# Two blocks on one core: a bias table's route, the split of a normed x, a gate's slots, and a pacing rate

## The chip, the cores and the metric

One of the eight cores of a Trainium2 chip runs the whole program in one launch. The metric is the device time of one execution in microseconds, as the median of several executions. Profiles show one execution, and their times count from the span's start.

## What is computed

`reference(...)` applies two transformer-like blocks to x of 256 tokens by 2048 features, all in float32.

```python
def reference(...):
    x = first_block(x, ...)      # mLSTM and gated delta rule side by side, gates, out projection, residual, rmsnorm
    return second_block(x, ...)  # below

def second_block(x, c, ctx, c_ctx, norm_g, w_mod, b_mod, w_in, w_out, lam_..., subln_g, rpb, final_g):
    shift, scale, gate = jnp.split(jax.nn.silu(c) @ wm + bm, 3, axis=-1)
    shift_c, scale_c = jnp.split(jax.nn.silu(c_ctx) @ wm[:, :2 * D_MODEL] + bm[:2 * D_MODEL], 2, axis=-1)
    hx = rmsnorm(h, norm_g[layer]) * (1.0 + scale[:, None]) + shift[:, None]
    hc = rmsnorm(ctx, norm_g[layer]) * (1.0 + scale_c) + shift_c
    qa, ka, va, ga, qb, kb, vb, gb = jnp.split(hx @ wi, 8, axis=-1)
    ...                                   # keys and values of hc too
    oa = diff_attention(...) * jax.nn.silu(ga)
    ob = neighbourhood_attention(..., rpb[layer], rows) * jax.nn.silu(gb)
    mixed = jnp.concatenate([oa, ob], axis=-1) @ w_out[layer]
    h = h + gate[:, None] * mixed
    return rmsnorm(h, final_g)
```

`hx` and `hc` have 256 rows each. `diff_attention` has 8 heads, each with two softmaxes; `neighbourhood_attention` has 8 heads and adds a bias by relative position, of 15 x 31 numbers per head (`rpb`).

## The kernel before

**Numbers and products.** Each float32 matrix is split into a high part in a reduced format and the low rest, `lo = w - hi`; a product is three matmuls, hi x hi, hi x lo, lo x hi. A weight tile is 512 KB (128 partitions of 1024 numbers). `load_w` loads it on SP's queue into one of four slots (pool wraw), and `split_w` makes `hi` with an ACT copy (line 139) and `lo` with a DVE subtraction (line 140) in three slots each (pool wsp). `proj` (line 161) multiplies eight weight tiles into a pair of PSUM banks (pool psA, two buffers), `proj_T` (line 145) does so for transposed results.

**Order.** The kernel is written in Tile: the code gives operations with priorities in their order of writing, and a planner puts them into each engine's in-order stream when their data and slots are there in its own timeline. Work written later fills gaps, so projections of the next stage run among the attention of the present one. `split_w` is raised in priority by 100. After each split `split_w` calls `tick[0]`, a hook that writes some side work at that point.

**Modulation.** The vectors shift, scale, gate need `silu(c) @ w_mod`, 12 column groups of 16 k tiles. `mod_step(i)` (line 460) is one of 192 steps: a load of 256 KB (line 463; for the last 64 on SP's queue) and a DVE multiply-add into a running sum (line 473). `mods(rate, upto)` (line 498) makes a hook that writes `rate` steps for each weight tile; `mods_all(upto)` writes what is still missing up to a number. The last 64 steps, the gate's, run in a ring of four slots and four sums, `mr`, and are paced from the first query tile of the neighbourhood attention on, at 1.6 a tile (line 1368). The four output columns of the last projection each call `mods_all(128 + 16 * (n + 1))` and `gate_row(n)`, which adds the sum over partitions with a matmul (`ms`, line 492), before column n is finished.

**Block 2's x.** After block 1, x lies as `hf[n]` (n = 0 to 3, 512 columns each, 256 rows). For each n, ACT scales it by the row norm (`xs`, line 941), PE transposes it in tiles of 128 (`ps`, line 945), and `mod_T` (line 857) applies scale and shift: ACT writes the high part `hxh` from PSUM, DVE writes the full value back to `hf[n]` from PSUM, and DVE (odd k) or POOL (even k) subtracts to give `hxl`. `value0` (line 988) then projects the values of hc and hx with `proj`, while `s_steps` (line 998) forms sums and differences of `hx` and `hc` quarters for a Strassen scheme, on DVE and ACT. `keys` (line 1048) uses these: it loads four weight tiles, forms differences of them on DVE (lines 1071 to 1074) and runs seven products; its first result goes to a scratch tile `tm` (line 1068).

**The bias table.** `rpb` is 8 rows of 465 numbers. It is loaded on POOL's queue to a tile `rb` of 8 partitions, one of two slots with the tag `tm`, and copied to DRAM as `rep`, 64 copies of every row (lines 971 to 973), from which `near_bias` (line 1299) later reads skewed windows. The other `tm` slot goes to `lq`.

**Attention.** `diff_attn(g, ...)` is called for two groups of four heads. `scores` writes two exponentials per head into a ring `er` of eight tiles of 512 columns; the next head's scores are written ahead of this head's `pv`. At the fourth unit it calls `gate2(g, "a")`, a projection with eight weight tiles whose result is turned into the gate `G` in a slot of its own (pool a2, one buffer); `out_T` transposes `G` at the end. `near_attn` follows with two groups, `gate2(g, "b")`, and writes `mb`, which takes the slot of `er`.

Of the kernel before, what the change touches and what calls it, by code (L numbers as in the profile page):

```python
# [9 lines left out]
F32 = mybir.dt.float32  # L10
F32R = mybir.dt.float32r
AF = mybir.ActivationFunctionType
ALU = mybir.AluOpType
# [3 lines left out]
P = 128  # L17
D = 2048
T = 256
# [65 lines left out]
def hybrid_block_kernel(  # L85
# [4 lines left out]
    act, ve, pe, gp = nc.scalar, nc.vector, nc.tensor, nc.gpsimd  # L90
# [29 lines left out]
    tick, last_lo = [None], [None]  # L120
# [79 lines left out]
    with ExitStack() as b1:  # L200
# [17 lines left out]
        with ExitStack() as s0:  # L218
# [64 lines left out]
            for w in range(2):  # L283
                for j in (1, 3):
                    for h in range(2):
                        hl = load_w(d["dn_qkv"][J0[w] + j, h], 8, P)
                        o = ps0[w][:, j // 2, j % 2, :]
# [20 lines left out]
            for n in range(4):  # L308
                full = pro.tile([P, 4, T], F32, tag="full", name="full", bufs=2)
                k4 = slice(4 * n, 4 * n + 4)  # L310
# [29 lines left out]
        with s1:  # L340
            nc.sync.dma_start(raws, d["if_ba"])
            ps = side([P, T], name="ps")[0:48]
            for h in range(2):
                hi, lo = split_w(raws[:, h * 8:(h + 1) * 8, :], 8, 48)
# [22 lines left out]
            e = gpool.tile([P, 2, 24], F32, name="e")  # L367
# [75 lines left out]
        for i, nm in enumerate(("c", "c_ctx")):  # L443
            o = VEC[nm]
# [3 lines left out]
        modT = cb1.tile([P, 4, KT], F32, name="modT")  # L448
# [49 lines left out]
        def mods(rate, upto):  # L498

            def f():  # L500
                mod_next[1] += rate
                while mod_next[1] >= 1.0:
                    mod_next[1] -= 1.0
                    if mod_next[0] < upto:
                        mod_step(mod_next[0])
                        mod_next[0] += 1
            return f
# [11 lines left out]
        with ExitStack() as s2:  # L519
# [38 lines left out]
            G = dn.tile([64, 8, 64], F32, name="G")  # L558
# [5 lines left out]
            for hg in range(4):  # L564
                vv, ww = (dn.tile([P, 2, 4, P], F32, tag=nm, name=nm) for nm in ("vv", "ww"))
                kq = dk.tile([P, 4, 2, T], F32, tag="kq", name="kq")
                ps = kps0 if hg == 0 else proj_T(d["dn_qkv"], 16 + 4 * hg, 4, U)
                rows = rsb if hg == 0 else None
                conv_silu(ps, 16 + 4 * hg, kq[:, :, 0, :], rows)
                ps = qps0 if hg == 0 else proj_T(d["dn_qkv"], 4 * hg, 4, U)  # L570
# [23 lines left out]
                for h in range(4):  # L594
                    g = 4 * hg + h
# [27 lines left out]
                for j in range(BASE - 1, 0, -1):  # L623
                    sh = [64, j, BASE - j]
# [9 lines left out]
                ps = proj_T(d["dn_qkv"], 32 + 4 * hg, 4, U)  # L634
# [19 lines left out]
                for q in range(4):  # L654
                    for i in range(8):
                        pe.matmul(cps[q % 2][Q[q], i, :], W[Q[q], i, :], Xd[Q[q], i, :], start=True, stop=True)
                    r = slice(32 * q, 32 * q + 16)
# [64 lines left out]
                st = sm1.tile([P, 2, 4], F32, tag="st", name="st")  # L722
# [23 lines left out]
        with ExitStack() as s3:  # L746
# [3 lines left out]
            for hg in range(2):  # L750
                kq = dk.tile([P, 4, 2, T], F32, tag="kq", name="kq")
                kT, qT = kq[:, :, 0, :], kq[:, :, 1, :]
                ps = proj_T(d["ml_k"], 4 * hg, 4, U)
                act.activation(kT, ps.rearrange("p a b t -> p (a b) t"), AF.Copy)  # L754
                ps = proj_T(d["ml_q"], 4 * hg, 4, U)
                act.activation(qT, ps.rearrange("p a b t -> p (a b) t"), AF.Copy, scale=P ** -0.5)
                for hp_ in range(2):
                    W0 = dk.tile([P, 2, T], F32, tag="W", name="W0")
                    W1 = ml.tile([P, 2, P], F32, tag="W1", name="W1")
                    for i in range(2):  # L760
                        h = 4 * hg + 2 * hp_ + i
# [54 lines left out]
                    for b in range(2):  # L816
# [4 lines left out]
                        for j in range(2):  # L821
                            k = 4 * (2 * hg + hp_) + 2 * b + j
# [10 lines left out]
        hf = [hfp.tile([P, 2, 512], F32, tag="hf", name="hf", bufs=4) for _ in range(4)]  # L833
# [3 lines left out]
        with ExitStack() as s4:  # L837
            o1 = s4.enter_context(tc.tile_pool(name="o1", bufs=2, reuse_waits="tile"))
            modp[0] = o1
            tick[0] = mods(0.55, 128)  # L840
            for n in range(4):
                gpp = proj(d["gate_a"], n, U)[0]
                act.activation(hf[n], gpp, AF.Tanh, scale=0.5)
            for n in range(4):
                gpp = proj(d["gate_b"], n, U)[0]
                act.activation(tb[:, :, n, :], gpp, AF.Tanh, scale=0.5)

            mods_all(128)
            tick[0] = None
            hch = big.tile([P, KT, T], F32R, tag="Ah", name="hch")  # L850
            hcl = big.tile([P, KT, T], F32R, tag="Al", name="hcl")
            gx = cb1.tile([P, 2, KT], F32, name="gx")
            og = VEC["norm_g"]
            for v in range(2):
                ve.scalar_tensor_tensor(gx[:, v, :], modT[:, 2 * v + 1, :], 1.0, vecT[:, og:og + 16], ALU.add, ALU.mult)

            def mod_T(ps, k, hi, lo, full):

                g, sh = gx[:, 0, k:k + 1], modT[:, 0, k:k + 1]
                act.activation(hi, ps, AF.Identity, scale=g, bias=sh)  # L860
                ve.tensor_scalar(full, ps, g, sh, ALU.mult, ALU.add)
                (ve if k % 2 else gp).tensor_tensor(lo, full, hi.bitcast(F32), ALU.subtract)

            for n in range(4):
                yp = proj(d["out_a"], n, [(hah, hal)])[0]
                ve.scalar_tensor_tensor(hf[n], hf[n], 1.0, yp, ALU.add, ALU.mult)
# [4 lines left out]
        with ExitStack() as s4:  # L871
# [66 lines left out]
            for n in range(4):  # L938
                xs = o1.tile([P, 2, 512], F32, tag="xr", name="xs")
                for t in range(2):  # L940
                    act.activation(xs[:, t, :], hf[n][:, t, :], AF.Copy, scale=rr[:, t:t + 1])
                for kk in range(4):
                    ps = side([P, T], name="ps")
                    for t in range(2):
                        pe.transpose(ps[:, t * P:(t + 1) * P], xs[:, t, kk * P:(kk + 1) * P], ident)
                    k = 4 * n + kk
                    mod_T(ps, k, hxh[:, k, :], hxl[:, k, :], hf[n][:, kk // 2, (kk % 2) * T:(kk % 2 + 1) * T])
            show("hxh", hxh.bitcast(F32))
        HX, HC = (hxh, hxl), (hch, hcl)

# [1 line left out]
    with ExitStack() as b2:  # L952
# [12 lines left out]
        with ExitStack() as s5:  # L965
# [2 lines left out]


            rep = tc.dram_tile([8, 64, 465], F32, name="rep")  # L970
            rb = st.tile([8, 465], F32, tag="tm", bufs=2, name="rb")
            gp.dma_start(rb, d["rpb"])
            gp.dma_start(rep, rb.rearrange("h (o n) -> h o n", o=1).to_broadcast([8, 64, 465]))


            lq = st.tile([P, 4, 64], F32, tag="tm", bufs=2, name="lq")
# [242 lines left out]

        def gate2(g, ab, G=None):  # L1220
            gp_ = proj(d["g" + ab], g, [HX])[0]
            if G is None:
                G = a2.tile([P, 2, 512], F32, tag="G", name="G", bufs=1)
            act.activation(G, gp_, AF.Tanh, scale=0.5)
            ve.scalar_tensor_tensor(G, G, 1.0, gp_, ALU.add, ALU.mult)
            return G
# [21 lines left out]
        def diff_attn(g, kT, V, qT, qlo):  # L1248
            S0 = [small.tile([P, 4, 2], F32, tag="s0", name="s0") for _ in range(2)]

            def scores(t, h):

                es, s0 = [], S0[t]
                for i in range(2):
                    sp = side([P, 512], name="sp")
                    pe.matmul(sp, qT[:, i, h, t * P:(t + 1) * P], kT[:, i, h, :, :], start=True, stop=False)  # L1256
                    pe.matmul(sp, qlo[:, i, h, t * P:(t + 1) * P], kT[:, i, h, :, :], start=False, stop=True)  # L1257
                    nm = small.tile([P, 1], F32, tag="nm", name="nm", bufs=4)
                    ve.tensor_reduce(nm, sp, AX.X, ALU.max, negate=True)
                    e = er[:, en[0] % 8, :]  # L1260
                    en[0] += 1
                    act.activation(e, sp, AF.Exp, bias=nm, accum_out=s0[:, h, i:i + 1])
                    es.append(e)
                fl = small.tile([P, 1], F32, tag="fl", name="fl")
                ve.reciprocal(fl, s0[:, h, 1:2])
                ve.scalar_tensor_tensor(fl, fl, nlam, s0[:, h, 0:1], ALU.mult, ALU.mult)
                ve.scalar_tensor_tensor(es[1], es[1], fl, es[0], ALU.mult, ALU.add)
                return es[1]


            U_ = [(t, h) for t in range(2) for h in range(4)]
            nxt = scores(*U_[0])
            for n, (t, h) in enumerate(U_):
                e, nxt = nxt, scores(*U_[n + 1]) if n < 7 else None
                if h == 0:
                    o_ = side([P, 4, P], name="o_")
                pv(e, V, h, o_[:, h, :])
                if n == 3:
                    G = gate2(g, "a")
                if h < 3:  # L1280
                    continue
                s0 = S0[t]
                jk = a2.tile([P, 4, P], F32, tag="e", bufs=3, name="jk")
                act.activation(jk, o_, AF.Square)
                so = small.tile([P, 4], F32, tag="sob", name="so")
                ve.tensor_reduce(so, jk, AX.X, ALU.add)
                rs = small.tile([P, 4], F32, tag="rsb", name="rs")
                ve.reciprocal(rs, s0[:, :, 0])
                ve.tensor_tensor(so, so, rs, ALU.mult)
                ve.tensor_tensor(so, so, rs, ALU.mult)  # L1290
                ve.tensor_scalar(so, so, 1.0 / P, 1e-5, ALU.mult, ALU.add)
                pow_(so, so, mh[:, 0:4])
                ve.tensor_tensor(rs, rs, so, ALU.mult)
                for i in range(4):
                    s = G[:, t, i * P:(i + 1) * P]
                    ve.scalar_tensor_tensor(s, o_[:, i, :], rs[:, i:i + 1], s, ALU.mult, ALU.mult)
            out_T(G, mah, mal, 4 * g, sg)
# [67 lines left out]
        KV = [kv(g, "b", False) for g in range(2)]  # L1365
        mr = big.tile([P, 8, 512], F32, tag="Al", name="mr")
        modp[0] = Ring(mr)
        tick[0] = mods(1.6, 192)
        for g in range(2):
            qT = queries(g, "b", False)  # L1370
            if g == 0:
# [16 lines left out]
        hf = []  # L1388
# [123 lines left out]
```

## Time and profile before

| | us |
|---|---|
| median of 3 runs | 1951.36 |
| lowest, highest | 1949.53, 1959.79 |
| the profiled execution | 1957.53 |
| its span | 1955.8 |
| PE busy in it | 1903.5 |
| DVE, ACT, POOL busy | 1499.5, 925.5, 259.2 |
| mean granted clock of PE | 0.987 |

The span runs from the first to the last instruction of the program. PE is TensorE's matmuls, PEld its weight loads, DVE VectorE, ACT ScalarE, POOL GpSimd, SP SyncE. [...] Rows of stretches give the length, then the busy time of PE, PEld, DVE, ACT and POOL with their instructions, the granted clock, the busy share of the 16 DMA engines and their GB/s. A wait is written as the waiting operation, an arrow, and what released it.

### The profile page before, as it was taken

Reading aid. Unit: us, or ns where it says so; the run is one execution under the profiler, and the core shown is the slowest. Engines: PE = TensorE matmul, PEld = TensorE weight load, DVE = VectorE, ACT = ScalarE, POOL = GpSimd, SP = SyncE. Lnnn points to the kernel's source line nnn. Section 1 sums busy time; section 2 is a strip of 40 time slices with the busy share of each in tenths; the row PEclk is TensorE's granted clock in tenths of the full one; section 3 lists DMA queues with packets and bytes.
Section 4 is the critical chain, followed back from the end, with each engine's and each line's share of the span. In section 5 each row is a group of like instructions: output and inputs, shape, how many; then the busy total and the mean of one; then the engine's idle time right before and its main releaser. Section 6 shows DMA issues by size and latency. Waiting matters only on the chain. (4 is left out here: it accounts for less than half of the span.)

```text
span 1955.8 us, 31707 instructions
## 1 busy us (share of the span) xinstructions
PE 1903.5 (97%) x12358; PEld 1684.1 (86%) x12358; DVE 1499.5 (77%) x2161; ACT 925.5 (47%) x1236; POOL 259.2 (13%) x379
## 2 busy tenths in 40 slices
PE   9999999999999999999999999979999999999988
PEld 9999898989888898888888877779999988979776
DVE  6978686785648999789994477868787668878985
ACT  7645444453334444444444365633433455555553
POOL 1011010110101221112110000200000033201211
PEclk9999999999999999999999999989999999999999
DMA  8545454453546788678886577553433387547974
GB/s 294 172 163 168 150 179 147 147 172 124 176 161 213 243 258 271 212 242 274 277 274 236 193 256 240 170 145 115 149 129 121 130 270 193 183 138 278 297 246 162
DMA packets 124071, 389.54 MB, mean 199 GB/s; under 512 B 15544, under 2 KB 22120, under 8 KB 123408
## 3 DMA queue, kind: packets, MB, share of 16 engines
q1 hardware_dynamic: 95296, 314.44, 47.8%
q0 software_dynamic: 19392, 53.96, 9.6%
q10 hardware_dynamic: 9232, 19.11, 3.0%
q8 instruction: 97, 1.59, 0.3%
q14 instruction: 54, 0.44, 0.1%
HBM read 368.28 MB, written 16.03 MB: 196 GB/s over the span
## 5 line engine op out<-in xcount | busy, mean ns | idle before, releaser
L139 ACT ACTIVATE hi<-w 128x1024 fp32r<-128x1024 f32 (+1 forms) x535 | 558.9, 1047 | 746.6 <-PE pN L173 400.4
L140 DVE TENSOR_TENSOR lo<-w,hi 128x1024 fp32r<-128x1024 f32 (+1 forms) x535 | 647.2, 1212 | 261.0 <-ACT hi L139 257.9
L172 PE MATMUL pN<-lo,uh 128*128 128x512 f32 x768 | 306.0, 398 | 0.0
L171 PE MATMUL pN<-hi,uh 128*128 128x512 f32 x768 | 304.4, 397 | 0.0
L173 PE MATMUL pN<-hi,ul 128*128 128x512 f32 x768 | 304.2, 396 | 0.0
L156 PE MATMUL pT<-uh,hi 128*128 128x256 f32 x896 | 255.5, 285 | 2.2 <-ACT kq L754 1.9
L158 PE MATMUL pT<-uh,lo 128*128 128x256 f32 x896 | 256.6, 287 | 0.0
L157 PE MATMUL pT<-ul,hi 128*128 128x256 f32 x896 | 255.7, 285 | 0.0
L171 PEld LDWEIGHTS pN<-hi,uh 128*128 128x128 f32 x768 | 144.9, 189 | 33.9
L173 PEld LDWEIGHTS pN<-hi,ul 128*128 128x128 f32 x768 | 144.8, 189 | 33.2
L172 PEld LDWEIGHTS pN<-lo,uh 128*128 128x128 f32 x768 | 144.8, 189 | 33.2
L156 PEld LDWEIGHTS pT<-uh,hi 128*128 128x128 f32 x896 | 168.7, 188 | 5.2 <-ACT kq L754 2.1
L158 PEld LDWEIGHTS pT<-uh,lo 128*128 128x128 f32 x896 | 168.8, 188 | 2.9 <-issue 2.4
L473 DVE SCALAR_TENSOR_TENSOR ma<-m,sc,ma 128x512 f32<-128x512 f32 x240 | 171.0, 749 | 0.0
L157 PEld LDWEIGHTS pT<-ul,hi 128*128 128x128 f32 x896 | 168.8, 188 | 1.8 <-issue 1.2
L463 POOL DMA_DIRECT2D m<-in_w_mod_dram x128 | 69.5, 544 | 287.7 <-DVE ma L473 206.0
L139 ACT ACTIVATE hi<-TT 128x1024 fp32r<-128x1024 f32 x56 | 59.6, 1064 | 77.2 <-PE pK L1064 56.5
L140 DVE TENSOR_TENSOR lo<-TT,hi 128x1024 fp32r<-128x1024 f32 x56 | 68.4, 1222 | 22.1 <-ACT hi L139 21.6
L156 PE MATMUL pT<-hxh,hi 128*128 128x256 f32 x256 | 73.5, 287 | 2.2 <-ACT ra L1165 2.2
L158 PE MATMUL pT<-hxh,lo 128*128 128x256 f32 x256 | 73.1, 286 | 0.1
L157 PE MATMUL pT<-hxl,hi 128*128 128x256 f32 x256 | 73.0, 285 | 0.0
L172 PE MATMUL pN<-lo,hxh 128*128 128x512 f32 x160 | 66.7, 417 | 3.6 <-DVE lo L140 3.5
(726 smaller groups left out, 4075.4 us busy)
## 6 DMA issues: line engine op xcount, KB each, us to landing
w<-in_dn_qkv_dram SPq DMA_DIRECT2D x88, 512.0 KB, 3.2
m<-in_w_mod_dram POOLq DMA_DIRECT2D x128, 256.0 KB, 4.0
w<-in_dn_z_dram SPq DMA_DIRECT2D x32, 512.0 KB, 3.2
w<-in_ml_v_dram SPq DMA_DIRECT2D x32, 512.0 KB, 3.7
w<-in_ml_z_dram SPq DMA_DIRECT2D x32, 512.0 KB, 4.1
w<-in_ml_o_dram SPq DMA_DIRECT2D x32, 512.0 KB, 3.4
w<-in_gate_a_dram SPq DMA_DIRECT2D x32, 512.0 KB, 4.3
w<-in_gate_b_dram SPq DMA_DIRECT2D x32, 512.0 KB, 4.3
```

The source lines that it names most:

```text
L139: act.activation(hi, raw, AF.Copy)
L140: last_lo[0] = ve.tensor_tensor(lo, raw, hi.bitcast(F32), ALU.subtract)
L156: pe.matmul(o, hi[:, k, :], xh[:, kt, :], start=(kt == 0), stop=False)
L157: pe.matmul(o, hi[:, k, :], xl[:, kt, :], start=False, stop=False)
L158: pe.matmul(o, lo[:, k, :], xh[:, kt, :], start=False, stop=(kt == KT - 1))
L171: pe.matmul(ps[:, t, :], xh[:, kt, s], hi[:, k, :], start=(kt == 0), stop=False)
L172: pe.matmul(ps[:, t, :], xh[:, kt, s], lo[:, k, :], start=False, stop=False)
L173: pe.matmul(ps[:, t, :], xl[:, kt, s], hi[:, k, :], start=False, stop=(kt == KT - 1))
L463: (gp if g < 8 else nc.sync).dma_start(raw, d["w_mod"][g, kt])
L473: ve.scalar_tensor_tensor(a, raw, s, a, ALU.mult, ALU.add)
```

## The change

Four edits. The bias rows go to a tile `rb` of 128 partitions with a slot of its own, each row read 16 times from DRAM, and the copy to `rep` writes each partition's row four times. In the normed x of block 2, ACT alone reads PSUM and writes the full value to `hf[n]`; once per n one ACT copy makes four k of `hxh` and one DVE subtraction four k of `hxl`. `diff_attn`'s second call puts its gate into tiles 6 and 7 of `er`, and the ring of exponentials uses tiles 0 to 5. The last 64 modulation steps are written at 1.0 per weight tile.

```diff
@@ -854,13 +854,6 @@
             for v in range(2):
                 ve.scalar_tensor_tensor(gx[:, v, :], modT[:, 2 * v + 1, :], 1.0, vecT[:, og:og + 16], ALU.add, ALU.mult)
 
-            def mod_T(ps, k, hi, lo, full):
-
-                g, sh = gx[:, 0, k:k + 1], modT[:, 0, k:k + 1]
-                act.activation(hi, ps, AF.Identity, scale=g, bias=sh)
-                ve.tensor_scalar(full, ps, g, sh, ALU.mult, ALU.add)
-                (ve if k % 2 else gp).tensor_tensor(lo, full, hi.bitcast(F32), ALU.subtract)
-
             for n in range(4):
                 yp = proj(d["out_a"], n, [(hah, hal)])[0]
                 ve.scalar_tensor_tensor(hf[n], hf[n], 1.0, yp, ALU.add, ALU.mult)
@@ -944,7 +937,12 @@
                     for t in range(2):
                         pe.transpose(ps[:, t * P:(t + 1) * P], xs[:, t, kk * P:(kk + 1) * P], ident)
                     k = 4 * n + kk
-                    mod_T(ps, k, hxh[:, k, :], hxl[:, k, :], hf[n][:, kk // 2, (kk % 2) * T:(kk % 2 + 1) * T])
+                    act.activation(hf[n][:, kk // 2, (kk % 2) * T:(kk % 2 + 1) * T], ps, AF.Identity,
+                                   scale=gx[:, 0, k:k + 1], bias=modT[:, 0, k:k + 1])
+                k4 = slice(4 * n, 4 * n + 4)
+                v4 = lambda a: a.rearrange("p (a b) t -> p a (b t)", a=2)
+                act.activation(v4(hxh[:, k4, :]), hf[n], AF.Copy)
+                ve.tensor_tensor(v4(hxl[:, k4, :]), hf[n], v4(hxh[:, k4, :]).bitcast(F32), ALU.subtract)
             show("hxh", hxh.bitcast(F32))
         HX, HC = (hxh, hxl), (hch, hcl)
 
@@ -968,9 +966,11 @@
 
 
             rep = tc.dram_tile([8, 64, 465], F32, name="rep")
-            rb = st.tile([8, 465], F32, tag="tm", bufs=2, name="rb")
-            gp.dma_start(rb, d["rpb"])
-            gp.dma_start(rep, rb.rearrange("h (o n) -> h o n", o=1).to_broadcast([8, 64, 465]))
+            rb = st.tile([P, 465], F32, name="rb")
+            rpb = d["rpb"]
+            gp.dma_start(rb, bass.AP(tensor=rpb.tensor, offset=rpb.offset, ap=[[465, 8], [0, 16], [1, 465]]))
+            rv = rep.rearrange("h (r i) n -> (h r) i n", i=4)
+            gp.dma_start(rv, rb.rearrange("p (o n) -> p o n", o=1).to_broadcast([P, 4, 465]))
 
 
             lq = st.tile([P, 4, 64], F32, tag="tm", bufs=2, name="lq")
@@ -1257,7 +1257,7 @@
                     pe.matmul(sp, qlo[:, i, h, t * P:(t + 1) * P], kT[:, i, h, :, :], start=False, stop=True)
                     nm = small.tile([P, 1], F32, tag="nm", name="nm", bufs=4)
                     ve.tensor_reduce(nm, sp, AX.X, ALU.max, negate=True)
-                    e = er[:, en[0] % 8, :]
+                    e = er[:, en[0] % 6, :]
                     en[0] += 1
                     act.activation(e, sp, AF.Exp, bias=nm, accum_out=s0[:, h, i:i + 1])
                     es.append(e)
@@ -1276,7 +1276,7 @@
                     o_ = side([P, 4, P], name="o_")
                 pv(e, V, h, o_[:, h, :])
                 if n == 3:
-                    G = gate2(g, "a")
+                    G = gate2(g, "a", er[:, 6:8, :] if g else None)
                 if h < 3:
                     continue
                 s0 = S0[t]
@@ -1365,7 +1365,7 @@
         KV = [kv(g, "b", False) for g in range(2)]
         mr = big.tile([P, 8, 512], F32, tag="Al", name="mr")
         modp[0] = Ring(mr)
-        tick[0] = mods(1.6, 192)
+        tick[0] = mods(1.0, 192)
         for g in range(2):
             qT = queries(g, "b", False)
             if g == 0:
```

`v4` views four k of 256 as two rows of 512.

## Rows read from the trace of the kernel before

**Rows 1.** The page: busy us of each engine (share) and instructions.

```profile
PE 1903.5 (97%) x12358; PEld 1684.1 (86%) x12358; DVE 1499.5 (77%) x2161; ACT 925.5 (47%) x1236; POOL 259.2 (13%) x379
```

**Rows 2.** Stretches: length, engines' busy us (instructions), PEclk, DMA share, GB/s.

```profile
1260.00:1270.00 10.00, 6.89 (x24) 5.35 (x23) 10.00 (x14) 4.43 (x8) 3.97 (x8) 0.69 0.45 156
1280.00:1290.00 10.00, 3.56 (x31) 3.35 (x29) 0.00 (x0) 0.00 (x0) 0.00 (x0) 0.89 0.54 87
1290.00:1300.00 10.00, 4.63 (x20) 4.34 (x21) 8.73 (x11) 4.34 (x6) 0.57 (x1) 0.50 0.72 218
```

**Rows 3.** The same view, after PE's two long waits.

```profile
1264.60:1270.80 6.20, 6.06 (x14) 4.77 (x15) 6.20 (x10) 2.67 (x3) 3.94 (x7) 0.51 0.60 177
1294.60:1301.20 6.60, 5.83 (x25) 5.54 (x26) 6.60 (x9) 1.18 (x3) 0.00 (x0) 0.50 0.82 282
```

**Rows 4.** PE's waits over the span: total us, times, longest.

```profile
PE pK L1063 <- ACT tm L1068: 11.0, 1, 11.0
PE pN L173 <- DVE mb L188: 5.2, 2, 3.1
PE pN L173 <- DVE hxl L862: 3.1, 1, 3.1
```

**Rows 5.** Timeline around 1291: start, duration, operation, idle before.

```profile
1291.27 1.22 DVE L1072 TENSOR_TENSOR TT<-w 128x1024 f32<-128x1024 f32 x1 [12.11 <-DMA w<-in_ka_dram]
1294.60 0.58 PE L1063 MATMUL pK<-s4h,hi 128*128 128x256 f32 x1 [11.04 <-ACT tm L1068]
```

**Rows 6.** Line 1045's loads to landing: issued at 1272.4; three before.

```profile
DMA to landing us min/median/max: 18.9/18.9/18.9
DMA to landing us min/median/max: 3.2/3.2/3.8
```

**Rows 7.** The bias copy's issue; DMA issues 1271 to 1295, last to landing.

```profile
L973 POOL DMA_DIRECT2D rep<-rb x1: 864/864/864, 1271.6 to 1271.6; - x1
rep<-rb POOLq DMA_DIRECT2D x1, 930.0 KB, 22.5
vda<-stg POOLq DMA_DIRECT2D x2, 512.0 KB, 4.1
```

**Rows 8.** POOL's DMA queue, 1278 to 1290: packets, MB, engines' share.

```profile
q0 software_dynamic: 105, 0.59, 44.9%
```

**Rows 9.** Groups, 1235 to 1285: count, busy us, mean ns, idle before.

```profile
L860 ACT ACTIVATE hxh<-ps,modT,gx 128x256 fp32r<-128x256 f32 x16 | 7.7, 560 | 1.5 <-PE ps L945 1.5
L861 DVE TENSOR_SCALAR hf<-ps,gx,modT 128x256 f32<-128x256 f32 x16 | 7.7, 533 | 0.6 <-ACT hxh L860 0.6
L862 DVE TENSOR_TENSOR hxl<-hf,hxh 128x256 fp32r<-128x256 f32 x8 | 3.2, 413 | 0.0
L1020 DVE TENSOR_TENSOR hcl<-hcf,hch 128x1024 fp32r<-128x1024 f32 x2 | 2.4, 1214 | 0.0
L1015 ACT ACTIVATE hch<-hcf 128x1024 fp32r<-128x1024 f32 x2 | 2.1, 1062 | 0.5 <-DVE hcf L1002 0.5
```

**Rows 10.** Line 473 from 1600; DVE's waits 1780 to 1900; chain piece.

```profile
L473 DVE SCALAR_TENSOR_TENSOR mr<-mr,sc x60: 725/745/1786, 1780.6 to 1890.3; 128x512 f32<-128x512 f32 x60
DVE mr L473 <- DMA mr<-in_w_mod_dram: 8.2, 9, 2.2
1841.40 7.00 DMA mr<-in_w_mod_dram
```

**Rows 11.** Gate G's writes, 1615 to 1731; line 173, 1655 to 1672.

```profile
L1224 ACT ACTIVATE G<-pN x2: 1019/1026/1034, 1622.3 to 1729.5; 128x1024 f32<-128x1024 f32 x2
L173 PE MATMUL pN<-hi,hxl x16: 390/396/628, 1654.8 to 1669.6; 128*128 128x512 f32 x16
```

**Rows 12.** Stretches as in rows 2, attention and last columns.

```profile
1710.00:1730.00 20.00, 17.14 (x84) 14.00 (x83) 14.04 (x25) 9.99 (x18) 1.02 (x1) 0.83 0.44 157
1830.00:1900.00 70.00, 61.76 (x322) 49.49 (x321) 59.25 (x92) 37.06 (x69) 11.05 (x14) 0.98 0.83 273
1900.00:1930.00 30.00, 30.00 (x131) 24.34 (x130) 24.13 (x22) 16.17 (x21) 6.25 (x4) 1.00 0.71 228
```

## The prediction, made before the changed kernel ran

> **What bounds the kernel now.** I read the busy totals first: TensorE (PE) is busy 1903.5 us of a span of 1955.8 [rows 1], so a change can gain only where PE stands idle, 52.3 us in all, or runs at the lower clock. Next I read the busy time in stretches of ten microseconds, looking for stretches in which PE is far below full while another engine is full or everything is empty. One place stands out [rows 2]. From 1260 to 1270 VectorE (DVE) has no idle time and PE has 3.1 us of it; from 1280 to 1290 DVE, ScalarE (ACT) and GpSimd (POOL) do nothing at all, and PE is busy 3.56 us. PE's waits name the ends of both holes [rows 4]: 3.1 us for `hxl` (line 862, DVE) and 11.0 us for `tm` (line 1068, ACT). [...]
>
> What stood behind the 11.0 us? At 1291.27 DVE starts again, after 12.1 us, on the landing of an `in_ka` weight tile, and PE follows at 1294.60 [rows 5]. That tile was issued at 1272.38 and landed 18.9 us later; the three issued before it took 3.2 to 3.8 us [rows 6]. In between lies the bias copy `rep<-rb`: issued at 1271.6, 930 KB, 22.5 us from issue to landing [rows 7]. While it runs, its queue (q0) takes 44.9% of 16 DMA engines [rows 8], 7.2 engines' worth, for 0.59 MB in 12 us. So a copy out of 8 partitions keeps about eight engines busy and the weight tile's shares on those wait. Also `tm` takes turns with `rb` in two slots, and PE's wait for it ended just after the copy had landed (1271.6 + 22.5 = 1294.1).
>
> **The bias table.** The change gives the copy 128 source partitions, the same bytes, and `rb` a slot of its own. What is to be had: from 1280 to 1300 PE is idle 20 - 3.56 - 4.63 = 11.8 us [rows 2], and 5.83 us at half clock lose 2.9 [rows 3]: 14.7 us. What remains depends on the copy's new length, which no row shows. Upper bound: the same engine time on 16 engines. 0.449 x 16 x 12 us = 86 us for 0.59 MB, so 139 us for 0.95 MB (930 KB), 8.7 us on each of 16. Lower bound: the store `vda<-stg`, 128 partitions to DRAM on the same queue, 512 KB in 4.1 us [rows 7]. In proportion to bytes that store gives 7.4 us, and I take this, the row being nearest in kind. Before, the tile lost 18.9 - 3.8 = 15.1 us to a 22.5 us copy, a share of 0.67; of 7.4 us that is 5.0. The tile then lands at 1272.4 + 3.8 + 5.0 = 1281.2, and PE resumes about 3.3 us after the landing (1291.3 to 1294.6 [rows 5]), at 1284.5; it ran dry 11.0 us before 1294.6, at 1283.6. A hole of 0.9 us is left, with a margin 1.5, so the gain is 13.2. At the upper bound, with the whole 8.7 us in the way, PE resumes at 1288.2: 4.6 us idle and up to 2.9 for the clock, gain 7.2. At the lower it is 14.7. The wider load of `rb` is 128 rows in place of 8, on POOL's queue ahead of the copy and beside nothing that waits. POOL, freed of its subtractions (next part), may issue the copy earlier; it then meets another weight tile at the same price.
>
> [...]
>
> **Block 2's normed x.** Per group of four k before: four ACT scalings straight into `hxh`, four DVE tensor_scalar into `hf`, two DVE and two POOL subtractions. After: four ACT scalings into `hf` (same form and count, the cost kept), one ACT copy of 128x1024 and one DVE subtraction of 128x1024. DVE over the four groups [rows 9]: minus 7.7, minus 3.2, plus 4 x 1.214 = 4.9, so minus 6.0 us, in a stretch where DVE has none free [rows 2]. ACT gains 4 x 1.06 = 4.2 us and had 5.6 us free of ten there [rows 2]. POOL loses eight operations, and its queue reaches the `rb` load sooner. Against it: a k is now ready only with its group. PE had finished the last transposes when it ran dry, at 1264.6 - 3.1 = 1261.5 [rows 3, 4]. From there group 3 needs 4 x 0.56 + 1.06 + 1.21 = 4.5 us, to 1266.0. Meanwhile PE has group 2's two weight tiles, 24 matmuls at 0.23 us (131 in 30 us [rows 12]) or 5.5 us, to 1267.0. That covers it if group 2 is ready at 1261.5. Before, its last subtraction ended at 1264.6 in a full DVE; with three groups' saving (4.5 us) taken out and an operation 0.8 us longer put in, it ends near 1260.9. To be had: 3.1 idle and half of 6.06 us, together 6.1. I take 5. Bounds: 6.1, and minus 2 if each group comes one operation chain late and PE stops once more.
>
> **The second gate.** `G` has one slot in pool a2. ACT wrote it at 1622.3 and at 1729.5 [rows 11], the second time only after the transposes that read the first one, although the second gate's last matmuls began at 1669.6. So one of psA's two buffers was held for 60 us, and projections had one buffer. From 1710 to 1730 PE lost 2.9 us idle and, at a granted 0.83, about 17.1 x 0.17 = 2.9 more [rows 12]; most of the idle time is one wait of the scores for the exponential before them. With G in `er` 6 and 7 the gate can be read out about 1671, and projection matmuls may fill that hole. But DVE and ACT also had key splits of the next attention to do there, which stay. Bounds 5.8 and minus 1; I take 3. The ring of exponentials falls from 8 to 6 tiles. A head takes two and the code keeps two heads in flight, so four are in use; I cost it at nothing, and if the order ran three heads ahead, one wait of at most those 2.9 us would be its price. `mb` follows `er` in its slot; `er` is now read until the second gate's transposes, which end well before the next attention writes `mb`, so this too is free.
>
> **Modulation steps.** There are 64 steps (256 KB on SP's queue and a DVE operation of 0.745 us each [rows 10]) between 1780 and 1891. At 1.6 per weight tile their emission ends with tile 40 counted from the first query tile; at 1.0 it ends with tile 64: 16 of them are emitted after tile 48, in the last two output columns. From 1830 to 1900 PE is idle 8.2 us [rows 12], 5.2 of it waiting for `mb` (DVE line 188) [rows 4]. The chain of waits reaches both through steps that stood in DVE's queue on their own transfer, one of them 7.0 us [rows 10]. Fewer steps there would free up to 8 us with the clock. But I count less: 60 in 109.7 us is 1.83 us a step, so at 1850 about 38 had run, where only some 25 stood ahead of that `mb` in the code, so the planner already drops later steps into DVE's gaps, and it still can. Behind the splits and `mr` transfers are queued in SP's order; a step moved late stands before the splits of the last columns, where DVE has 30 - 24.1 = 5.9 us free [rows 12] and 16 x 0.745 = 11.9 us could come. Bounds 8 and minus 5; I take 2.
>
> **Sum.** 13.2 + 5 + 3 + 2 = 23.2 us. The profiled execution took 1957.5 us (span 1955.8), so 1934.3; it lies 6.2 above the median of the runs, and against the median the forecast is 1951.4 - 23.2 = 1928 us. PE, 97% busy [rows 1], passes an earlier start on.
>
> **Rivals.**
> 1. The copy stays as long as it was, limited by something that partitions don't widen. Only the wait on `tm` goes, and the weight tile lands as late as before. For: no row shows a wide copy of short rows. Against: the half share of the engines. Left: 5 + 3 + 2 = 10, 1941 us.
> 2. The two reorderings late in the kernel give nothing back: gate minus 1, steps minus 5 because the last gate row comes late. 13.2 + 5 - 6 = 12, 1939 us. For: DVE is 80% busy in the output columns. Against: PE has no idle there now [rows 12].
> 3. Slower: the 16 late steps stand in DVE's in-order queue ahead of the splits and each waits for its transfer as long as the longest of the nine such waits, 2.2 us [rows 10]. 16 x 2.2 = 35 us less 23 is plus 12: 1963 us. It turns the sign from 23.2 / 16 = 1.45 us a step. Against: the nine waits make 8.2 us over 60 steps.
> 4. The changed plan opens as many new holes as it closes, and nothing measurable is left: 1950 us.
>
> **How the numbers follow.** Forecast 0.70, rivals 0.10, 0.13, 0.03 and 0.04. The best of all bounds is 14.7 + 6.1 + 5.8 + 8 = 34.6, 1917 us; the runs before spread over ten microseconds. Range 1914 to 1945, which takes in rivals 1 and 2. About 0.5%, 9.8 us, is what a measurement of this kernel can tell from no change: faster means under 1941.6. Faster: 0.70, three quarters of rival 2 and half of rival 1, 0.86. Slower: 0.03. Same: 0.11.
>
> **What would show it.** Right: the copy lands in 4 to 10 us; no `in_ka` landing over 10 us; no stretch after 1250 with DVE and ACT both empty; PE's wait on `hxl` under 1 us; granted clock near 1.00 from 1260 to 1300; G's second tanh more than 40 us earlier. Wrong: a hole of over 5 us at the first `pK`, a clock at 0.50 after it, new PE waits on `lo` (line 140) or on `ms` in the last 60 us.

## The result, and the profile after

The changed kernel took 1931.08 us beside 1954.38 for the kernel before on the same chip: ratio 0.9876, interval 0.9834 to 0.9917. (The 1931.08 is the median of four executions, of which one, of 4771 us, was disturbed and is not in the ratio; the other three took 1928.47, 1928.52 and 1933.63.) A second set of runs on another chip gave a median of 1934.59, ratio 0.9896 [0.9881, 0.9911]. So some 20 to 24 us are saved; the forecast was 23.2 and 1928 us. The profiled execution took 1928.5 us, where the sum had 1934.3.

The busy line and the stretches come first, as in [rows 1, 2] (length, busy us of PE, PEld, DVE, ACT and POOL, granted clock, DMA share, GB/s):

```profile
PE 1892.6 (98%) x12358; PEld 1676.7 (87%) x12358; DVE 1491.6 (77%) x2141; ACT 928.7 (48%) x1240; POOL 256.7 (13%) x371
...
1250.00:1260.00 10.00, 9.51 (x49) 7.66 (x49) 10.00 (x10) 10.00 (x17) 2.92 (x5) 1.00 0.75 179
1260.00:1270.00 10.00, 8.23 (x35) 6.06 (x33) 10.00 (x10) 9.58 (x11) 0.56 (x1) 1.00 0.82 246
1270.00:1280.00 10.00, 9.94 (x61) 8.93 (x62) 10.00 (x12) 4.46 (x6) 0.54 (x1) 1.00 0.58 186
1280.00:1290.00 10.00, 10.00 (x87) 10.00 (x87) 10.00 (x12) 3.35 (x4) 0.00 (x0) 1.00 0.48 182
1290.00:1300.00 10.00, 10.00 (x87) 10.00 (x86) 7.90 (x12) 4.36 (x5) 0.55 (x1) 1.00 0.65 224
```

The empty stretch of [rows 2] is gone: from 1280 to 1300 PE has no idle time where it had 11.8 us, and the clock is at 1.00 in all five stretches. A second profile of the same kernel, from the runs on the other chip, has no idle time from 1280 to 1300 either, but 3.4 us at the lower clock before that:

```profile
1271.40:1274.80 3.40, 3.40 (x9) 2.62 (x8) 3.40 (x5) 0.60 (x1) 0.00 (x0) 0.50 0.66 242
```

PE's waits in the first profile (us in total, times, longest), to be laid beside [rows 4]:

```profile
PE pN L172 <- DVE lo L140: 7.7, 7, 2.0
PE tp L1237 <- ACT eT L1234: 2.7, 5, 0.7
PE tp L1232 <- ACT e L1331: 2.3, 3, 1.2
...
PE pK L1063 <- ACT hi L139: 1.0, 1, 1.0
```

No wait on `tm` and none on `mb` is left; the one on `hxl` is 0.5 us, where [rows 4] had 3.1. Two small ones follow it, for split weight tiles: 1.0 us on `hi` (line 139) and 0.9 of the 7.7 on `lo` (line 140), so that PE is idle 1.8 us from 1260 to 1270, where it was 3.1. Another 3.0 us on `lo` lie in the last 60 us, where the kernel before has none; the prediction had named them as a sign of being wrong, and the part on the steps comes back to them.

The copy and the weight tiles around it, as in [rows 6, 7] (POOL's issue with its start and duration; KB and us to landing; then line 1045's five loads from 1261.0 to 1274.8, shortest, median and longest):

```profile
1254.71 0.78 POOL L973 DMA_DIRECT2D rep<-rb  x1
...
rep<-rb POOLq DMA_DIRECT2D x1, 930.0 KB, 8.9
...
DMA to landing us min/median/max: 3.1/3.3/6.6
```

The copy lands in 8.9 us instead of 22.5, and is issued 16.9 us earlier than in [rows 7], because POOL no longer stands in the subtractions of the normed x. No `in_ka` tile takes longer than 6.6 us.

Where the time came from is seen by setting the same operations of the two traces side by side:

| operation starts at, us (last two rows: ends) | before | after | gained so far |
|---|---|---|---|
| 7937th matmul of PE, among the first of `pK` | 1277.8 | 1275.5 | 2.3 |
| first matmul of `pV` | 1369.3 | 1351.9 | 17.4 |
| first scores `sp` of `diff_attn` | 1627.3 | 1606.3 | 21.0 |
| first scores of the neighbourhood attention | 1784.3 | 1763.1 | 21.2 |
| last `mb` | 1888.8 | 1857.5 | 31.3 |
| last matmul of PE | 1946.4 | 1917.3 | 29.1 |

The first row takes the same matmul by its count, because the very first `pK` starts 8.9 us earlier only by going ahead of 23 matmuls of the values. Most of the gain is there by the first `pV`, in the place that the prediction named: 15.1 us come between the first two rows, at the hole behind the bias copy. From there to the first scores 3.6 us more appear, but that stage was not changed, and the kernel with nothing but a slot for `rb` (below), which saves nothing, gains 3.2 there too; so they seem to lie in the one profile of the kernel before. The `diff_attn` stage takes as long as before, but PE does 37 matmuls more in it (length, then as in [rows 2], first before and then after):

```profile
1627.30:1784.30 157.00, 152.10 (x1006) 138.39 (x1005) 122.75 (x193) 88.45 (x145) 26.48 (x31) 0.97 0.57 175
1606.30:1763.10 156.80, 155.82 (x1043) 142.39 (x1043) 126.96 (x198) 91.72 (x148) 26.94 (x31) 1.00 0.60 185
```

These are done ahead of the neighbourhood attention, which is 10.1 us shorter up to the last `mb`. The last steps belong to two single executions: the second profile of the changed kernel has 0.6 us in the first row, 15.8 at the first `pV`, 20.5 and 19.6 at the first scores of the two attentions, 26.2 at the last `mb` and 24.1 at the last matmul. Two executions of one program differ by some 5 us in the late attention, so below about that the stage is judged by the timed runs alone.

### The profile page after: what moved, and what is told of

Read it like the earlier page. It is cut to its first block, busy times and chain, and to the rows that moved or that the text cites. A ratio compares the mean times of both kernels' runs of the same rounds, so it can differ in the third digit from the quotient of the medians.

```text
span 1926.6 us, 31678 instructions
## 1 busy us (share of the span) xinstructions
PE 1892.6 (98%) x12358; PEld 1676.7 (87%) x12358; DVE 1491.6 (77%) x2141; ACT 928.7 (48%) x1240; POOL 256.7 (13%) x371
## 5 line engine op out<-in xcount | busy, mean ns | idle before, releaser
L139 ACT ACTIVATE hi<-w 128x1024 fp32r<-128x1024 f32 (+1 forms) x535 | 559.1, 1047 | 711.3 <-PE pN L173 393.5
```

The source lines that it names most:

```text
L139: act.activation(hi, raw, AF.Copy)
```

## The experiments

The edits are shown against the kernel before where a part is made alone, and against the changed kernel where one is left out. They ran in three sets, each on one chip together with runs of the kernel before (1956.2, 1955.4 and 1955.8 us). Savings are (1 - ratio) x 1955.5 us.

| kernel | ratio, 95% interval | saved, us |
|---|---|---|
| whole change, again | 0.9896 [0.9881, 0.9911] | 20.3 |
| all but the bias table | 0.9959 [0.9941, 0.9977] | 8.0 |
| all but the normed x | 0.9913 [0.9895, 0.9930] | 17.0 |
| all but the gate (two sets) | 0.9872 [0.9857, 0.9888]; 0.9877 [0.9860, 0.9893] | 25.0; 24.1 |
| all but the steps | 0.9897 [0.9880, 0.9915] | 20.1 |
| bias table alone | 0.9920 [0.9906, 0.9934] | 15.6 |
| normed x alone | 0.9985 [0.9972, 0.9998] | 2.9 |
| gate alone | 1.0002 [0.9988, 1.0015] | -0.4 |
| steps alone | 0.9983 [0.9974, 0.9992] | 3.3 |
| bias table and normed x | 0.9909 [0.9889, 0.9929] | 17.8 |
| `rb` in a slot of its own, 8 partitions | 1.0004 [0.9994, 1.0014] | -0.8 |

**All but the bias table.**

```diff
-            rb = st.tile([P, 465], F32, name="rb")
+            rb = st.tile([8, 465], F32, tag="tm", bufs=2, name="rb")
...
-            gp.dma_start(rv, rb.rearrange("p (o n) -> p o n", o=1).to_broadcast([P, 4, 465]))
+            gp.dma_start(rep, rb.rearrange("h (o n) -> h o n", o=1).to_broadcast([8, 64, 465]))
```

> The changed kernel with the old bias table (8 partitions, sharing tm's slots); split, gate and rate as changed. Theory: the copy takes about 22 us again, one in_ka weight tile lands after more than 12 us, PE idles over 8 us at the start of the keys and runs at half clock after it: 13 to 15 us slower than the changed kernel, ratio to the kernel before about 0.995. Rival: the split alone gives DVE enough lead to cover the late tile; then under 5 us slower, ratio about 0.99.

It saved 8.0 us, so the bias table is worth 12.3 to 16.2 in the whole change (20.3 or 24.2 less 8.0). In its trace: POOL's issue; the copy; the three `in_ka` tiles issued from 1261.4 to 1270.5; and PE's longest wait.

```profile
1255.26 0.86 POOL L971 DMA_DIRECT2D rep<-rb  x1
...
rep<-rb POOLq DMA_DIRECT2D x1, 930.0 KB, 22.7
...
DMA to landing us min/median/max: 12.9/18.4/19.5
...
PE pK L1061 <- ACT hi L139: 13.9, 1, 13.9
```

Here the copy out of 8 partitions is issued as early as in the changed kernel, and still takes 22.7 us. Now three tiles are late instead of one, and the hole is 13.9 us. So issuing early doesn't remove the hole; the copy's length makes it. The wait no longer names `tm` but line 139, which reads the late weight tile.

**A slot of its own, and nothing else.**

```diff
-            rb = st.tile([8, 465], F32, tag="tm", bufs=2, name="rb")
+            rb = st.tile([8, 465], F32, name="rb")
```

> The kernel before with one edit: rb in a slot of its own, still 8 partitions. Theory: the hole is the late weight tile's; the copy still takes about 22 us, a tile lands after 15 us or more, PE's hole at the first keys stays at 9 to 12 us, at most 1.5 us faster, ratio 0.999 to 1.000. Rival: PE's wait is on tm, as the profile names it, and tm waits for the copy out of the shared slot; without sharing the hole falls under 6 us, 6 us or more faster, ratio 0.997 or less.

No gain: 1.0004. PE's wait and the copy in its trace, then the `in_ka` tile that is issued 0.8 us after the copy:

```profile
PE pK L1063 <- ACT tm L1068: 10.2, 1, 10.2
...
rep<-rb POOLq DMA_DIRECT2D x1, 930.0 KB, 22.5
...
DMA to landing us min/median/max: 18.1/18.1/18.1
```

`rb` can no longer hold a slot of `tm`, and the profile names `tm` as before. That wait was a follower of the weight tile, and the rival cause, the shared slot, falls. (The wide copy in a shared slot wasn't tried.)

**The bias table alone.** This is its part of the diff put into the kernel before.

> The kernel before with one edit: rb on 128 partitions in a slot of its own. Theory: the copy takes 7 to 10 us, no in_ka tile lands after more than 10 us, the hole at the first keys shrinks from 11 us to under 3; hxl's wait and its half clock stay; 12 to 16 us faster, ratio 0.992 to 0.994. Rival: with the old split DVE is the bound behind the hole and 5 us or more of it stay; ratio 0.996 or more.

15.6 us saved, with an interval of 2.7 either way. POOL, still busy with subtractions, issues the copy at 1271.7, as late as in [rows 7]; this is the case that the prediction had worked out:

```profile
rep<-rb POOLq DMA_DIRECT2D x1, 930.0 KB, 9.2
...
PE pN L173 <- DVE hxl L862: 3.4, 2, 3.1
PE pK L1067 <- DVE lo L140: 3.1, 2, 2.0
PE pK L1065 <- ACT tm L1070: 0.5, 1, 0.5
```

The copy takes 9.2 us, the slowest of line 1047's `in_ka` loads 8.3, and the `pK` waits are 3.6 us together, where the forecast left 0.9 to 1.5 and the upper bound 4.6.

**All but the normed x.**

```diff
-                act.activation(v4(hxh[:, k4, :]), hf[n], AF.Copy)
-                ve.tensor_tensor(v4(hxl[:, k4, :]), hf[n], v4(hxh[:, k4, :]).bitcast(F32), ALU.subtract)
+                    mod_T(ps, k, hxh[:, k, :], hxl[:, k, :], hf[n][:, kk // 2, (kk % 2) * T:(kk % 2 + 1) * T])
```

> The changed kernel with the old mod_T (two PSUM reads per k, subtraction per k on DVE and POOL); bias, gate and rate as changed. Theory: PE waits 2 to 4 us for hxl again and falls to half clock, 4 to 6 us slower than the changed kernel, ratio to before about 0.991. Rival: once the bias copy is out of the way the DVE backlog has nobody waiting, under 1 us slower, ratio 0.988.

17.0 us saved, so the normed x is worth 3.3 to 7.2 in the whole change. The stretch after the last transposes, and PE's waits there, are those of the kernel before [rows 3, 4]:

```profile
1264.60:1270.80 6.20, 6.20 (x15) 4.95 (x16) 6.20 (x10) 2.81 (x3) 4.08 (x7) 0.53 0.61 204
...
PE pN L173 <- DVE hxl L862: 3.1, 1, 3.1
PE pK L1065 <- ACT tm L1070: 1.1, 1, 1.1
```

**The normed x alone.**

> The kernel before with one edit: the four-k split of the normed x. Theory: hxl's wait goes, but PE and POOL reach the narrow bias copy and its late tiles sooner, so the hole at the first keys grows from 11 us to 13 or 14; 2 to 5 us faster, ratio 0.9975 to 0.999. Rival, as counted in the forecast's first rival: its 5 to 7 us stay whole, ratio 0.9965 to 0.9975.

2.9 us saved. The trace has PE at its first `pV` 2.4 us earlier, because the bias copy, still from 8 partitions, now makes a hole of 14.1 us where there were 11.0:

```profile
PE pK L1061 <- ACT hi L139: 14.1, 1, 14.1
```

So 3.1 us of what it frees are handed to the next hole, and appear only where that is closed too.

**The gate alone.**

```diff
-                    e = er[:, en[0] % 8, :]
+                    e = er[:, en[0] % 6, :]
...
-                    G = gate2(g, "a")
+                    G = gate2(g, "a", er[:, 6:8, :] if g else None)
```

> The kernel before with one edit: the second gate in er's tiles 6 and 7, ring of 6. Theory, from the run without the gate edit (ratio 0.9872, as the changed kernel's): the tanh moves over 40 us earlier and the hole near 1714 closes, but PE loses as much later in the attention; ratio 0.998 to 1.001. Rival, as forecast: 3 to 6 us stay, ratio 0.997 to 0.9985.

Nothing: 1.0002 [0.9988, 1.0015]. Three stretches, first of the kernel before and then of this one:

```profile
1700.00:1740.00 40.00, 37.13 (x216) 32.19 (x215) 28.13 (x48) 21.85 (x35) 1.02 (x1) 0.91 0.49 166
1800.00:1840.00 40.00, 39.64 (x217) 33.45 (x215) 38.56 (x57) 23.16 (x40) 13.43 (x16) 1.00 0.91 293
1840.00:1900.00 60.00, 52.12 (x270) 41.45 (x269) 49.49 (x78) 31.89 (x58) 8.07 (x10) 0.97 0.83 274
```

```profile
1700.00:1740.00 40.00, 40.00 (x236) 34.88 (x235) 29.95 (x47) 24.08 (x37) 1.02 (x1) 1.00 0.56 197
1800.00:1840.00 40.00, 34.74 (x187) 28.45 (x185) 36.66 (x58) 21.44 (x42) 14.23 (x19) 0.96 0.94 289
1840.00:1900.00 60.00, 55.62 (x282) 44.59 (x281) 52.19 (x80) 32.46 (x60) 11.21 (x12) 0.97 0.80 264
...
PE tp L1232 <- ACT e L1331: 3.9, 3, 1.4
...
PE hp L1245 <- DVE G L1344: 2.3, 1, 2.3
```

The first stretch does what was said of it: the second gate's tanh starts at 1677.5 instead of 1729.5 [rows 11], the 2.9 idle us and the lower clock are gone, and PE issues 20 matmuls more. From 1800 to 1840 it issues 30 fewer and stands idle 5.3 us instead of 0.4, in waits for the exponentials and for their transposes (`e` and `eT`, line 1234). From 1840 to 1900 it is busy 3.5 us more: the waits for `mb` are gone, and one of 2.3 us for the last gate (`G`) has come.

The same exchange shows in all six profiles of kernels with this edit, beside the eight without it. From the first scores of `diff_attn` to those of the neighbourhood attention PE starts 1043 to 1046 matmuls instead of 1004 to 1008, and in the 40 us that begin 15 us after the latter it is busy 34.4 to 35.5 us instead of 38.1 to 39.9. The projections that fill PE beside the neighbourhood attention have been used up earlier. So the hole is closed, and time is given back later; that nothing is left on balance is told by the timed runs, since single profiles differ too much there.

**All but the gate.** Twice, in two sets, since the first came out as fast as the whole change.

> The changed kernel with the old ring of 8 exponentials and G in its one slot. Theory: the second gate's tanh again comes only after the first gate's transposes, PE idles 2 to 3 us with a lower clock near 1690 to 1710, 3 to 6 us slower than the changed kernel, ratio to before about 0.990. Rival: the held PSUM buffer costs nothing because other projections fill PE, under 1 us slower, ratio 0.988.

> Bias, split and rate with the old gate slot, a second time, because it came out ahead of the whole change once (0.9872 against 0.9896 and 0.9876). Theory: the gate's slots are worth nothing either way, ratio 0.988 to 0.990. Rival: they cost 3 to 5 us, ratio 0.986 to 0.9875.

25.0 and 24.1 us saved, beside 24.2 and 20.3 with the gate. The 3 to 6 us of loss that were expected at first did not come, and the second ratio lies between the ranges of its theory and its rival. Leaving the gate out costs nothing and may save some microseconds; the intervals overlap. The trace of the second shows the same exchange from the other side: PE busy 27.16 us of 30 from 1680 to 1710, at a clock of 0.94, against 30.00 with the gate, and then 49.71 of 50 from 1770 to 1820 against 45.52.

**The modulation steps alone.**

```diff
-        tick[0] = mods(1.6, 192)
+        tick[0] = mods(1.0, 192)
```

> The kernel before with one edit: 1.0 modulation steps a tile. Theory: the steps leave the attention, PE's waits for mb (5.2 us) go, and a third of that comes back in the last columns: 3 to 6 us faster, ratio 0.997 to 0.9985. Rival, as forecast: the planner fills the gaps at either rate, 0 to 2 us, ratio 0.999 to 1.000.

3.3 us saved, with an interval of 1.8 either way. In its trace the wait for `mb`, and the stretches of [rows 12]:

```profile
PE pN L173 <- DVE mb L188: 1.6, 1, 1.6
...
1830.00:1900.00 70.00, 65.67 (x336) 52.90 (x335) 57.09 (x87) 37.66 (x66) 11.91 (x13) 0.98 0.81 267
```

PE is busy 65.67 of these 70 us, where it was 61.76; the wait for `mb` falls from 5.2 to 1.6 us. The 60 steps now lie between 1777.8 and 1913.5, 135.7 us instead of 109.7 [rows 10]. In the last columns, 1900 to 1930, PE is busy 29.91 of 30 us with the late steps in DVE's queue: their price, which two rivals rested on, isn't seen in this kernel.

It is seen where the gate's edit is made too. In the changed kernel four steps stand in DVE's queue between two splits of late weight tiles, and PE waits for the second `lo` (start, duration and operation on DVE, then on PE; last PE's waits of this kind in the last 60 us):

```profile
1864.40 2.33 DVE L473 SCALAR_TENSOR_TENSOR mr<-mr,sc 128x512 f32<-128x512 f32 x3
...
1867.84 0.74 DVE L473 SCALAR_TENSOR_TENSOR mr<-mr,sc 128x512 f32<-128x512 f32 x1
1868.50 1.22 DVE L140 TENSOR_TENSOR lo<-w,hi 128x1024 fp32r<-128x1024 f32 x1
...
1869.77 0.50 PE L172 MATMUL pN<-lo,mah 128*128 128x512 f32 x1 [1.23 <-DVE lo L140]
...
PE pN L172 <- DVE lo L140: 3.0, 3, 1.3
```

All four profiles of kernels with both edits have such waits there, 2.0 to 3.0 us; those with one of the two, or with neither, have 0 to 0.2.

**All but the steps**, and **the bias table with the normed x**.

> The changed kernel with 1.6 modulation steps a tile again. Theory as forecast: the planner fills DVE's gaps with steps at either rate, 0 to 3 us slower than the changed kernel, ratio to before 0.988 to 0.990. Rival, from the trace of the changed kernel (its last mb comes 31 us earlier, the attention before it only 19 us earlier): the rate is worth 8 us or more, PE again waits 4 to 6 us for mb, ratio to before 0.992 or more.

> Bias and split, with the old gate slot and the old rate. Theory: nearly all of the gain is here, the gate and the rate edits give 0 to 3 us together; ratio 0.989 to 0.991. Rival, as forecast: gate and rate carry 5 us; ratio 0.992 or more.

Without the steps 20.1 us are saved, so they are worth 0.2 to 4.1 beside the gate. Bias table and normed x together save 17.8, near the 18.5 of the two alone. On the same chip, adding the steps to those two (which is all but the gate) saves 24.1, 6.3 more. This kernel's `mb` waits, 6.6 us, are the ones that the steps take away:

```profile
PE pN L173 <- DVE mb L188: 6.6, 2, 3.5
```

The gate takes them away too: in none of the six profiles with its edit, with the steps or without, does PE wait for this `mb` of DVE. So the two edits work on the same wait, and their savings can't be added.

**The whole change, again.**

> The changed kernel once more, beside the next three and the kernel before on the same chip. Both theories: ratio 0.985 to 0.990; it is the yardstick for the single edits.

0.9896 [0.9881, 0.9911]; the four parts alone sum to 15.6 + 2.9 - 0.4 + 3.3 = 21.4 us, beside its 20.3 and the first set's 24.2. On the whole nothing large lies in how the parts act on each other, though gate and steps overlap.

## Why the prediction was right, point by point

**The place and the cause** were right. PE's idle time at 1280 to 1300 came from a weight tile behind a bias copy that took 22.5 us; the five kernels tried that keep the 8 partitions have a copy of 22.4 to 22.9 us and a hole of 10.2 to 14.1; all that spread it have at most 3.6 us of waits at `pK`, with a copy of 8.9 us (the whole change), 9.2 (alone), 9.3 (without the gate) and 10.3 (without the normed x). Of the signs that the prediction had set, all that spoke for it came in the first profile (the second gate's tanh, for one, starts at 1656.1 instead of 1729.5), and of those against it one did: the waits on `lo` in the last 60 us.

**The bias term** was 13.2 us; alone it measured 15.6 +- 2.7, left out 12.3 to 16.2. One step inside it failed, and another made good for it. The copy was taken at 7.4 us and takes 8.9 to 10.3, past the upper bound of 8.7. But that bound had the wrong reason: it kept the engine time per byte. This is POOL's queue while the wide copy's own packets run, 1258.2 to 1261.8 (packets, MB, share of 16 engines), with SP's queue below it:

```profile
q0 software_dynamic: 210, 0.96, 86.4%
q1 hardware_dynamic: 56, 0.20, 15.9%
```

0.864 x 16 x 3.6 us is 50 us of engine time for 0.96 MB, 52 per MB, where [rows 8] gave 86 us for 0.59 MB, 146 per MB. So in these two copies a byte out of 128 partitions took 0.36 of the engine time of one out of 8, and the packets are through in 3.6 us. The rest of the 8.9 us is 3.5 us between the issue and the first packet and 1.8 after the last one, which the forecast's bounds had not set apart; how long the copy would be with the engines to itself, no run shows. The old copy moved 0.59 MB in the 12 us of [rows 8], 49 GB/s, the wide one 0.96 MB in 3.6 us, 267 GB/s; why its bytes take less engine time, no run shows.

The residue then followed the copy's issue. Issued late it leaves `pK` waits of 3.6 us (bias table alone) and 2.2 (all but the normed x), between the forecast's 0.9 and the bound's 4.6. Issued early, because POOL is freed, it meets tiles that nobody waits for as closely, and 1.0 us is left. The prediction had said that an earlier copy would meet another tile "at the same price"; that was too dear.

**The normed x** was 5 us: 3.3 to 7.2 when left out, with the wait on `hxl` down from 3.1 to 0.5 us. Alone it gives 2.9, for the reason seen above. But the size came true in part by another way than the forecast's, and that is luck. In its own place, up to the 7937th matmul, the changed kernel gains 2.3 us, and 0.6 in the second profile: the waits on `hi` and `lo`, and there the lower clock, take the rest. What is left comes through the copy that POOL issues earlier: from that matmul to the first `pV` the changed kernel gains 15.1 us and the one without the normed x 12.3. The forecast had given the earlier copy no worth.

**The gate** was 3 us and is worth 0 alone and nothing that can be told from zero beside the other parts. The term was mis-sized, and the step that failed is that matmuls filling the hole at 1710 to 1730 were counted as a gain. The hole closes as said; but the matmuls that close it are those that stood later beside the neighbourhood attention, which then lacks them. The low bound, minus 1, and the second rival named the direction. The ring of six cost nothing that shows.

**The steps** were 2 us and measured 3.3 +- 1.8 alone, 6.3 added to bias table and normed x, 0.2 to 4.1 beside the gate. The term was mis-sized by the step that the planner already drops late steps into DVE's gaps "and it still can": the rate does decide when they run, 136 us of spread instead of 110, and the waits for `mb` go with it. The price that the low bound counted, late steps ahead of the splits, is there beside the gate, as up to 3.0 us.

**The sum** came out right partly because errors nearly cancel: for gate and steps the forecast was 3 + 2 and alone they measured -0.4 + 3.3; for the first two terms it was 13.2 + 5 and alone they measured 15.6 + 2.9, 17.8 together. One slip stands in the chances: 0.70, three quarters of 0.13 and half of 0.10 make 0.85, not 0.86.

**The rivals.** A copy as long as before (1) is refuted by 8.9 us. Reorderings that give nothing back (2) hold for the gate and, made alone, not for the steps. Late steps that each wait for their transfer (3): DVE's waits for these transfers are 7.4 us at line 473 and 5.0 at line 471, beside 8.2 [rows 10] and 2.1 before; the rival needed 35. As many new holes as old (4) happened in one part only.

**What stays open.** Gate and steps act on the same stretch, the late attention: all but the gate is as fast as the whole. Whether the whole change loses a few microseconds to its gate can't be settled here: the two differ by -0.1 to 4.7 us, by which sets are compared, and the intervals are of that size. The 3.0 us of waits on `lo`, which come only with both edits, speak for such a loss; they were not removed in a run. No kernel of these is shown to be faster than the whole change.

## What to carry to other kernels

Where all engines but the DMA stand still, look for the long transfer that runs beside the late one (here a copy of 22.5 us beside a tile that took 18.9), and not only at the tile that the wait names: a buffer named as the releaser can be a follower of the load that is really late, which one run with a slot of its own tells. Before counting a hole filled by work from later as a gain, look whether the later stage has other work to put there. And a hole at the front hands what an edit frees ahead of it to itself, so an edit's worth alone and its worth beside the others are two numbers.

## What the runs showed of the hardware

In these runs a DMA out of 8 partitions delayed loads of another queue almost until its own end or past it. In the kernel before, the tile issued at 1272.4 took 18.9 us beside 3.2 to 3.8 for the three before it, and landed at 1291.3, 2.8 us before the copy [rows 6, 7]. With the copy issued earlier (all but the bias table) three loads took 12.9 to 19.5 us, and the last of them, issued at 1270.5, landed at 1283.4 or later, over 5 us after the copy (1255.3 + 22.7 = 1278.0). The copy's packets took 0.449 x 16 x 12 us / 105 = 0.82 us each [rows 8]. How a DMA engine divides its time between two queues, no run shows, so why the loads lose that much stays open.

The lower clock after a short hole is no fixed price. After the same 3.1 us wait on `hxl` the granted clock was 0.51 in the kernel before [rows 3] and 0.53 in the kernel without the normed x, but 1.00 from 1266 to 1272 in the one with the bias table alone and in the one with a slot for `rb`; the former is:

```profile
1266.00:1272.00 6.00, 5.64 (x25) 4.29 (x24) 6.00 (x9) 5.71 (x6) 5.11 (x9) 1.00 0.72 174
```

And after the same waits of 1.0 and 0.9 us the changed kernel kept 1.00 in its first profile and fell to 0.50 in its second, as shown with the result. So the 3 us that the forecast counted for the clock there may or may not be had by closing the hole. Why it differs, the runs don't show.
